# SwiGLU's gate and up matrices: the low part of the first weight tile by a subtraction on VectorE in place of a negated copy and an adding transfer

## The chip, the cores and the metric

The kernel runs on one core of a Trainium2 chip. The metric is device time in microseconds (us), the median of several runs of the whole program. The profile is one further execution, taken by the hardware profiler. The engines are TensorE (PE, matmuls), VectorE (DVE), ScalarE (ACT), GpSimd (POOL) and SyncE (SP). Each engine works off its own instructions in the order in which they were queued; semaphores tie the engines together. In this kernel SP issues plain transfers between HBM (main memory) and SBUF (on-chip memory), and GpSimd issues the adding ones.

## The reference, cut to what matters

One layer of a hybrid decoder runs on 576 tokens of width 1024: a mixer (Mamba-2 and mLSTM heads), cross attention to a memory, and a SwiGLU block. The change concerns the last one:

```
u = _rms(x) * g_pre_ffn                             # 576 x 1024
f = (jax.nn.silu(u @ w_gate) * (u @ w_up)) @ w_down # hidden width 2816 = 22 tiles of 128
x = x + _rms(f) * g_post_ffn
```

All data is float32.

## The kernel before, in words

**Three products for one.** TensorE multiplies in the type float32r, which keeps fewer bits than float32. So each operand is split into a high part (a cast to float32r) and a low part (the rest, operand minus high part), and each product is made of three: high by high, high by low, low by high. In `mul` (from line 1721 on) these are lines 1725, 1726 and 1727; line 1727 is the one that reads the low part of the weights.

**Seven products for eight.** From hidden tile 4 on, the gate and up matrices are taken in pairs of tiles (j, j+1). A pair is one weight matrix of two tiles, cut in half along its 1024 inputs (columns LA and LB of an SBUF tile); the tokens are cut in halves of 288 and the inputs in halves of 512. The 2 by 2 blocks are multiplied with seven products (w = 0 to 6) after Strassen and Winograd, not eight; each is 12 matmuls. A pair therefore needs, besides the raw tiles r1 (tile j, name `raw`) and r2 (tile j+1, name `rawx`), sums and differences of their halves, each split into high and low parts:

- `load`: r2 is fetched, and the low part l1 of r1 is made in a buffer named `wacc` (two of them). Before the change: ScalarE writes the negated, rounded r1 (line 1666), and a transfer on GpSimd's queue adds r1 from HBM to it (line 1667), which leaves r1 minus its high part.
- `high1`: ScalarE casts r1 to its high part h1 (line 1671), in one of three buffers `whi`. For five pairs, marked `first`, the low part is made here by VectorE's subtraction in one of three buffers `wlo` (line 1674), and not in `load`.
- `sums`, `diffs`: VectorE forms sums and differences, in `sw` and in place in r1 and r2 (lines 1677 to 1686). Line 1686 overwrites half of r1.
- `parts2`, `place3`, `parts3`, `parts4`: high and low parts of these. `place3` takes a half tile's low part by the negated copy and the adding transfer too, into `wlo`.
- products 0 and 1 use h1, l1; 2 and 3 the sums' parts; 4 and 5 the third parts; 6 the fourth. When `parts4` is through, r1's buffer (two of them) is free for the first tile of the next pair but one.

`early` runs products 0 and 1, `mid` 2 to 4, `late` 5 and 6. Between them ScalarE copies a half-finished sum out of its PSUM bank (cc of lines 1782 and 1793, ct of line 1789), since TensorE adds the next product onto the same bank; TensorE has to wait for that copy.

**Order.** The pairs are 6 to 20 in steps of two, first gate, then up. Pairs made by `pairs` are ordered by the framework's planner, which runs a model of time over the steps and puts each engine's instructions in a fixed order. After the pairs for tiles 6 and 8, and again after those for 10, 12 and 14, comes a stage of the down projection, `down_blocks` (from line 1946 on), with four blocks of the same kind (`Down`). There the order is written out by hand: `on(t, ...)` gives every step a place t, and the steps are queued in the order of t. The stage begins while the last gate and up pair (g_ and u in the code) is still in work, and ends with the first pair of the next group. The steps of block 0 stand in one list, which the change edits. In a `Down` block `low1` (lines 1867 to 1870) makes the low part by negated copy and adding transfer, `low1v` by a subtraction on VectorE; `diff1` overwrites part of the raw tile; `high4` and `low4` are the fourth parts. The names `keep`, `plus`, `done` empty PSUM banks; L1994 and L2002 are two such copies for u, in cc and ct.

Of the kernel before, what the change touches and what calls it, by code (L numbers as in the profile page):

```python
# [12 lines left out]
F32R = mybir.dt.float32r  # L13
# [6 lines left out]
P = 128  # L20
# [96 lines left out]
def build(nc, tc, ctx, I, O):  # L117
# [4 lines left out]
    wp = ctx.enter_context(tc.tile_pool(name="weights", bufs=1))  # L122
# [548 lines left out]
    for g in range(2):  # L671
        for hb in range(2):
            dst = cpad[:, g, 4 * hb:4 * hb + 4, :].rearrange("p b t -> p (b t)")
# [5 lines left out]
    for g in range(2):  # L679
# [13 lines left out]
        for h in range(8):  # L693
            k, j = h % 2, (8 * g + h) // 2
# [125 lines left out]
    for h in range(4):  # L820
        q, k = qk[:, h, :], qk[:, 4 + h, :]
# [607 lines left out]
    def load(key, src):  # L1429
        W[key] = wp.tile([P, 1024], F32, name="raw", tag="raw", bufs=2)  # L1430
        S.dma_start(W[key], src)
# [165 lines left out]
    for n_, (key, p) in enumerate(order):  # L1597
        src = I[{"xo": "wxo", "g": "wgate", "u": "wup"}[key[0]]][key[1]]
        at_(order[n_ - 2][1] + 0.01 if n_ > 1 else -1, load, key, src)
        if key[1] == 3:  # L1600
            at_(p, cast3, n_)
            at_((0.55, 1.05)[n_], low3, n_)
        else:
            at_(p, cast, key, PRE.index(key), wx if key in (("g", 0), ("u", 0), ("g", 1)) else None)
# [40 lines left out]
    class Pair:  # L1645

        def __init__(s, j, up, dst):
            s.j, s.up, s.dst, s.first = j, up, dst, j in (10, 16) or (j, up) == (6, 1)
            s.src = I["wup" if up else "wgate"]
            s.r1 = wp.tile([P, 1024], F32, name="raw", tag="raw", bufs=2)  # L1650
            S.dma_start(s.r1, s.src[j])

        def load(s):
            s.r2 = fp.tile([P, 1024], F32, name="rawx", tag="rawx", bufs=2)
            S.dma_start(s.r2, s.src[s.j + 1])
            if s.first:
                return
            s.l1 = fp.tile([P, 1024], F32R, name="wacc", tag="wacc", bufs=2)
            s.low(s.l1, s.r1, s.j)

        def low(s, out, raw, j, c=slice(0, 1024)):

# [6 lines left out]
        def high1(s):  # L1669
            s.h1 = wp.tile([P, 1024], F32R, name="whi", tag="whi", bufs=3)  # L1670
            A.copy(s.h1, s.r1)
            if s.first:
                s.l1 = wp.tile([P, 1024], F32R, name="wlo", tag="wlo", bufs=3)
                V.tensor_tensor(s.l1, s.r1, s.h1.bitcast(F32), op=ALU.subtract)

        def sums(s):
# [163 lines left out]
    class Down:  # L1840
# [29 lines left out]
            G.dma_start(s.f1[1], I["wdown"][s.j, :, 768 * s.c - 256:768 * s.c + 512], accum_op=ALU.add)  # L1870

        def high1(s):
            if s.n == 1:
                s.f1 = s.parts()
            A.copy(s.f1[0], s.r1)

# [69 lines left out]
    def down_blocks(c, up_gate, j):  # L1946
# [4 lines left out]
        def on(t, fn, *a):  # L1951
            ev.append((t, len(ev), lambda: fn(*a)))
# [56 lines left out]
        on(2.8, up_mul, u, "z", 6, b22, False)  # L2009
        on(4.5, lambda: u.done(0, 1, u.z, ct[:, 0, :]))  # L2010

        for k, p in (("low1", -11.3), ("sum1", -11.0), ("sum2", -10.5), ("diff2", -9.9), ("high1", -7.95), ("diff1", -7.1),
                     ("high3", -6.3), ("low3", -5.5), ("high4", -4.6), ("low4", -4.1), ("high2", -1.5), ("low2", -0.7)):
            on(p, do, 0, k)
        on(-9.0, make, 1)
        on(-8.9, do, 1, "load")
# [119 lines left out]
    with tc.manual_schedule(engines={TE.engine, A.engine, V.engine, G.engine, S.engine}):  # L2136
# [4 lines left out]
        fp = ctx.enter_context(tc.tile_pool(name="ffn", bufs=1, reuse_waits="tile"))  # L2141
# [7 lines left out]
    w_of = lambda j: weights(("d", j), I["wdown"][j, :, 0:512], 512, cut=512)  # L2149
    down_chunk(0, 4, [(j, i) for j in range(8) for i in (1, 0)], pp[1], w_of, ev_first)  # L2150
    made = down_blocks(1, pairs((6, 8), operand, whole=False), 10)
    made = down_blocks(2, pairs((10, 12, 14), operand, None, made, False), 16)
    hh, hl = SL0("hh2"), SL(2, "hl2", F32R)
    f2 = SL(4, "f_ffn")
# [257 lines left out]
```

## Time and profile before

| what | value |
|---|---|
| median of 3 runs | 1135.39 us (1132.99 to 1137.53) |
| the profiled execution | 1135.51 us, of which its span 1133.7 us |
| mean granted TensorE clock | 0.994 |
| TensorE matmuls busy | 1101.4 us, 97% of the span |
| VectorE busy | 758.1 us, 67% |
| ScalarE busy | 618.7 us, 55% |
| GpSimd busy | 233.9 us, 21% |
| pairs 6 on and down blocks | about 803 to 1077 us of the span |

By stretches of that part, from the view of windows (the first numbers are the window and its length; then the busy time with the number of instructions of PE, PEld, DVE, ACT and POOL; then the mean granted TensorE clock, the share of time in which the DMA engines were busy, and GB/s):

```
803.00:864.00 61.00, 57.36 (x425) 56.05 (x425) 39.53 (x69) 37.83 (x70) 6.85 (x8) 1.00 0.66 165
864.00:918.00 54.00, 51.59 (x382) 50.34 (x380) 40.45 (x73) 28.70 (x50) 12.03 (x14) 1.00 0.78 171
918.00:974.00 56.00, 52.74 (x382) 52.04 (x383) 41.75 (x81) 36.62 (x68) 5.96 (x7) 0.97 0.58 134
974.00:1038.00 64.00, 59.34 (x436) 57.62 (x435) 45.48 (x81) 34.19 (x59) 13.01 (x16) 0.99 0.84 210
1038.00:1077.00 39.00, 38.78 (x273) 38.78 (x274) 24.47 (x45) 23.91 (x42) 4.26 (x5) 0.92 0.52 116
```

How to read the rows of a timeline: start in us, duration, engine, line of the code, operation, output<-inputs, shapes, count, and in brackets the idle time of the engine just before with what ended it ("[3.16 <-ACT cc L1793]": 3.16 us idle, until ScalarE's instruction of line 1793 on cc was through). Matmuls overlap in the pipeline, so their durations exceed their spacing; TensorE's speed is read from the starts. The clock is a share of full speed.

### The profile page before, as it was taken

Reading aid. Unit: us, or ns where it says so; the run is one execution under the profiler, and the core shown is the slowest. Engines: PE = TensorE matmul, PEld = TensorE weight load, DVE = VectorE, ACT = ScalarE, POOL = GpSimd, SP = SyncE. Lnnn points to the kernel's source line nnn. Section 1 sums busy time; section 2 is a strip of 40 time slices with the busy share of each in tenths; the row PEclk is TensorE's granted clock in tenths of the full one; section 3 lists DMA queues with packets and bytes.
Section 4 is the critical chain, followed back from the end, with each engine's and each line's share of the span. In section 5 each row is a group of like instructions: output and inputs, shape, how many; then the busy total and the mean of one; then the engine's idle time right before and its main releaser. Section 6 shows DMA issues by size and latency. Waiting matters only on the chain.

```text
span 1133.7 us, 21313 instructions
## 1 busy us (share of the span) xinstructions
PE 1101.4 (97%) x8355; PEld 1047.8 (92%) x8355; DVE 758.1 (67%) x1508; ACT 618.7 (55%) x1143; POOL 233.9 (21%) x322
## 2 busy tenths in 40 slices
PE   9999999999999999999999999999999999998997
PEld 8999889898998999999988889999998989998997
DVE  6796874457777775659654545684577767775655
ACT  6877533356554475656454445544665566555644
POOL 1333443313122212100244202100011211121000
PEclk9999999999999999999999999999999999998999
DMA  6685555544563448753567765723764974597542
GB/s 207 161 167 128 135 163 168 149 106 126 168 181 105 129 158 294 265 209 96 200 214 251 275 209 180 254 84 104 211 140 88 224 170 122 117 249 180 129 139 84
DMA packets 62456, 191.00 MB, mean 168 GB/s; under 512 B 6892, under 2 KB 11116, under 8 KB 61844
## 3 DMA queue, kind: packets, MB, share of 16 engines
q1 hardware_dynamic: 44324, 142.19, 37.6%
q0 software_dynamic: 17744, 46.93, 20.8%
q8 instruction: 65, 1.06, 0.4%
q10 hardware_dynamic: 288, 0.52, 0.1%
q14 instruction: 35, 0.29, 0.1%
HBM read 160.31 MB, written 29.30 MB: 167 GB/s over the span
## 4 chain that ended last, share of the span: by engine, by line
PE 79%; DMA 9%; ACT 5%; DVE 4%; issue 2%; SPq 0%; DVEq 0%; ACTq 0%
PE ps_in L201 5%; PE ps_in L203 5%; PE ps_in L202 5%; PE ps_o L201 3%; PE ps_o L203 2%; PE ps_u L1725 2%; PE ps_o L202 2%; PE ps_u L1726 2%; PE ps_u L1727 2%; PE ps_g L1725 2%; PE ps_g L1726 2%; PE ps_g L1727 2%; PE ps_dn L1932 2%; PE ps_dn L201 2%; PE ps_dn L1931 2%; PE ps_dn L203 2%
## 5 line engine op out<-in xcount | busy, mean ns | idle before, releaser
L201 PE MATMUL ps_in<-uh,whi 128*128 128x320 f32 (+1 forms) x544 | 165.5, 304 | 0.0
L203 PE MATMUL ps_in<-uh,wlo 128*128 128x320 f32 (+1 forms) x544 | 163.0, 300 | 0.5 <-DVE wlo L188 0.5
L202 PE MATMUL ps_in<-ul,whi 128*128 128x320 f32 (+1 forms) x544 | 162.4, 299 | 0.0
L181 ACT CAST whi<-raw 128x1024 fp32r<-128x1024 f32 (+1 forms) x102 | 102.9, 1011 | 80.9 <-PE ps_in L202 19.5
L188 DVE TENSOR_TENSOR wlo<-raw,whi 128x512 fp32r<-128x512 f32 (+1 forms) x94 | 87.9, 935 | 59.6 <-ACT whi L181 58.7
L201 PEld LDWEIGHTS ps_in<-uh,whi 128*128 128x128 f32 x544 | 103.1, 190 | 2.5 <-issue 0.8
L203 PEld LDWEIGHTS ps_in<-uh,wlo 128*128 128x128 f32 x544 | 103.0, 189 | 2.4 <-issue 1.3
L202 PEld LDWEIGHTS ps_in<-ul,whi 128*128 128x128 f32 x544 | 103.2, 190 | 0.7
L1725 PE MATMUL ps_u<-b,whi 128*128 128x288 f32 x144 | 43.8, 304 | 9.6 <-ACT cc L1793 3.2
L186 POOL DMA_DIRECT2D wlo<-win x32 | 28.3, 885 | 94.6 <-ACT wlo L185 84.1
L1725 PE MATMUL ps_g<-b,whi 128*128 128x288 f32 x144 | 42.9, 298 | 1.2 <-ACT cc L1793 1.0
L1726 PE MATMUL ps_u<-b,whi 128*128 128x288 f32 x144 | 43.1, 299 | 0.0
L1726 PE MATMUL ps_g<-b,whi 128*128 128x288 f32 x144 | 42.5, 295 | 0.0
L201 PE MATMUL ps_o<-mixm_h,whi 128*128 128x256 f32 (+1 forms) x128 | 38.8, 304 | 1.7 <-ACT whi L181 1.6
L201 PE MATMUL ps_xo<-qh,whi 128*128 128x288 f32 x128 | 37.9, 301 | 1.0 <-ACT f_xo L1407 1.0
L202 PE MATMUL ps_o<-mixm_l,whi 128*128 128x256 f32 (+1 forms) x128 | 38.6, 302 | 0.0
L203 PE MATMUL ps_o<-mixm_h,wlo 128*128 128x256 f32 (+1 forms) x128 | 38.3, 303 | 0.0
L201 PE MATMUL ps_xq<-u2h,whi 128*128 128x320 f32 (+1 forms) x128 | 38.3, 303 | 0.0
L774 PE MATMUL ps_v<-wlo,uh 128*128 128x256 f32 x128 | 36.8, 291 | 1.4 <-DMA wlo<-wv 1.3
L202 PE MATMUL ps_xq<-u2l,whi 128*128 128x320 f32 (+1 forms) x128 | 38.0, 299 | 0.0
L203 PE MATMUL ps_xq<-u2h,wlo 128*128 128x320 f32 (+1 forms) x128 | 37.9, 297 | 0.0
L203 PE MATMUL ps_xo<-qh,wlo 128*128 128x288 f32 x128 | 37.9, 297 | 0.0
(779 smaller groups left out, 3933.0 us busy)
## 6 DMA issues: line engine op xcount, KB each, us to landing
raw<-win SPq DMA_DIRECT2D x35, 512.0 KB, 3.8
raw<-wout SPq DMA_DIRECT2D x17, 512.0 KB, 4.7
kva<-kc SPq DMA_DIRECT2D x16, 512.0 KB, 6.3
kva<-vc SPq DMA_DIRECT2D x16, 512.0 KB, 6.8
raw<-wxq SPq DMA_DIRECT2D x13, 512.0 KB, 3.6
raw<-wgate SPq DMA_DIRECT2D x13, 512.0 KB, 5.7
raw<-wup SPq DMA_DIRECT2D x13, 512.0 KB, 3.6
wlo<-win POOLq DMA_DIRECT2D x24, 256.0 KB, 5.5
```

Source lines behind the costliest of these rows:

```text
L181: A.copy(hi[:, :n], raw[:, :n])
L186: G.dma_start(lo[:, a:b], src[:, a:b], accum_op=ALU.add)
L188: e.tensor_tensor(lo[:, a:b], raw[:, a:b], hi[:, a:b].bitcast(F32), op=ALU.subtract)
L201: mm(ps, wh, ah, start=i == 0, stop=False)
L202: mm(ps, wh, al, start=False, stop=False)
L203: m = mm(ps, wl, ah, start=False, stop=i == len(tiles) - 1)
L774: m = mm(o, ah, lo[:, j:j + 256], start=False, stop=k == KT - 1, skip_group_check=True)
L1725: mm(ps, wh, b[0][:, k, :], start=start and k == 0, stop=False, skip_group_check=True)
L1726: mm(ps, wh, b[1][:, k, :], start=False, stop=False, skip_group_check=True)
L1727: m = mm(ps, wl, b[0][:, k, :], start=False, stop=k == 3, skip_group_check=True)
L1931: mm(ps, wh, bh, start=start and k == 0, stop=False, skip_group_check=True)
L1932: mm(ps, wh, bl, start=False, stop=False, skip_group_check=True)
```

## The change

The low part l1 of the first tile of each pair from tile 6 on is made by VectorE from the raw tile and its high part. The negated copy on ScalarE and the adding transfer of 512 KB on GpSimd's queue go for the eleven pairs that had them; only pair 4 keeps its old way (its low part is fetched ready-made). Pairs 10 and 16, gate, which are made inside the hand-written order, keep their buffer `wlo`; all others use `wacc`, among them 6, 10 and 16, up, which had `wlo` before and, no longer being `first`, are now prepared in the common order (`place3` ahead of `high1`). In the down stage, block 0 goes the same way: `low1` (place -11.3) is replaced by `low1v` (-4.2), `diff1` moves from -7.1 to -4.1, `high4` from -4.6 to -2.8, `low4` from -4.1 to -2.4, and the two buffers are taken at `high1`. The half tile in `place3` and the blocks 2 and 3 of the down stage keep the negated copy and the adding transfer.

```diff
-            s.j, s.up, s.dst, s.first = j, up, dst, j in (10, 16) or (j, up) == (6, 1)
+            s.j, s.up, s.dst, s.first = j, up, dst, not up and j in (10, 16)
...
-            if s.first:
-                return
-            s.l1 = fp.tile([P, 1024], F32R, name="wacc", tag="wacc", bufs=2)
-            s.low(s.l1, s.r1, s.j)
+            if s.j == 4:
+                s.l1 = fp.tile([P, 1024], F32R, name="wacc", tag="wacc", bufs=2)
+                s.low(s.l1, s.r1, s.j)
...
             A.copy(s.h1, s.r1)
-            if s.first:
-                s.l1 = wp.tile([P, 1024], F32R, name="wlo", tag="wlo", bufs=3)
+            if s.j > 4:
+                pool, tag, n = (wp, "wlo", 3) if s.first else (fp, "wacc", 2)
+                s.l1 = pool.tile([P, 1024], F32R, name=tag, tag=tag, bufs=n)
                 V.tensor_tensor(s.l1, s.r1, s.h1.bitcast(F32), op=ALU.subtract)
...
-            if s.n == 1:
+            if s.n < 2:
                 s.f1 = s.parts()
...
-        for k, p in (("low1", -11.3), ("sum1", -11.0), ("sum2", -10.5), ("diff2", -9.9), ("high1", -7.95), ("diff1", -7.1),
-                     ("high3", -6.3), ("low3", -5.5), ("high4", -4.6), ("low4", -4.1), ("high2", -1.5), ("low2", -0.7)):
+        for k, p in (("low1v", -4.2), ("sum1", -11.0), ("sum2", -10.5), ("diff2", -9.9), ("high1", -7.95), ("diff1", -4.1),
+                     ("high3", -6.3), ("low3", -5.5), ("high4", -2.8), ("low4", -2.4), ("high2", -1.5), ("low2", -0.7)):
```

## The prediction

> **What bounds the kernel now.** TensorE carries nearly the whole span, so I read first, for the stretch in which the changed pairs run (803 to 1077 us of the span), what TensorE waited for.
>
> ```profile
> PE ps_u L1725 <- ACT cc L1793: 3.2, 1, 3.2
> PE ps_u L1725 <- ACT ct L2002: 3.1, 2, 1.6
> PE ps_g L1725 <- ACT whi L1671: 2.5, 2, 2.1
> PE ps_u L1725 <- ACT cc L1994: 2.4, 2, 1.2
> PE ps_u L1727 <- DVE wlo L193: 1.1, 2, 0.8
> PE ps_g L1725 <- ACT cc L1793: 1.0, 2, 0.5
> PE ps_u L1725 <- ACT whi L192: 0.9, 1, 0.9
> ```
>
> The columns are the sum in us, the number of times and the longest. They come to 14.2 us, and all but 1.1 us is put down to ScalarE. ScalarE is busy for little more than half of the span, so the question is what it stood at. That is the second view, the waits of ScalarE in the same stretch:
>
> ```profile
> ACT wacc L1666 <- DMA raw<-wgate: 14.2, 6, 5.0
> ACT wacc L1666 <- DMA raw<-wup: 12.9, 5, 5.6
> ...
> ACT whi L1671 <- PE ps_g L1726: 5.2, 6, 1.1
> ```
>
> For 27.1 us, in all eleven of its uses, ScalarE stood at the negated copy of the first weight tile until that tile had arrived. The third view is the timeline around the longest wait; ScalarE first, then TensorE:
>
> ```profile
> 1036.83 1.06 ACT L1666 ACTIVATE wacc<-raw 128x1024 fp32r<-128x1024 f32 x1 [2.86 <-DMA raw<-wgate]
> 1037.79 0.38 ACT L1793 COPY cc<-ps_u 128x288 f32<-128x288 f32 x1
> ```
>
> ```profile
> 1038.22 0.61 PE L1725 MATMUL ps_u<-b,whi 128*128 128x288 f32 x1 [3.16 <-ACT cc L1793]
> ```
>
> The small copy of line 1793, which empties a bank for TensorE, stands in ScalarE's queue behind a negation that waits for a weight tile of a later pair (20, gate). The next worst is the same, with the cast of line 1671 behind the negation for (14, up):
>
> ```profile
> 915.17 1.06 ACT L1666 ACTIVATE wacc<-raw 128x1024 fp32r<-128x1024 f32 x1 [5.61 <-DMA raw<-wup]
> ...
> 916.80 1.03 ACT L1671 CAST whi<-raw 128x1024 fp32r<-128x1024 f32 x1
> ```
>
> ```profile
> 917.88 0.61 PE L1725 MATMUL ps_g<-u3h,whi 128*128 128x288 f32 x1 [2.08 <-ACT whi L1671]
> ```
>
> The smaller waits in the pairs (0.4 us of line 1671, 0.9 of line 192, 0.8 of line 193) lie within 5 us behind two more such stands:
>
> ```profile
> 829.35 1.06 ACT L1666 ACTIVATE wacc<-raw 128x1024 fp32r<-128x1024 f32 x1 [3.32 <-DMA raw<-wup]
> ...
> 1015.48 1.06 ACT L1666 ACTIVATE wacc<-raw 128x1024 fp32r<-128x1024 f32 x1 [5.03 <-DMA raw<-wgate]
> ```
>
> So what ends last at these places is a load, but not because the matmuls need it: the copy was queued too early.
>
> The fourth view is the granted clock behind the two long waits:
>
> ```profile
> 917.90:921.30 3.40, 3.40 (x14) 3.40 (x15) 2.99 (x5) 2.92 (x7) 0.85 (x1) 0.50 0.95 146
> 921.30:924.70 3.40, 3.40 (x28) 3.40 (x27) 2.81 (x5) 1.71 (x3) 0.00 (x0) 1.00 0.97 216
> ...
> 1038.20:1044.10 5.90, 5.88 (x24) 5.88 (x25) 2.42 (x5) 3.14 (x5) 1.68 (x2) 0.50 0.78 128
> ```
>
> The first pair of numbers is the window and its length, the next TensorE's busy time with its matmuls, the last three the clock, the DMA share and GB/s. Behind each long wait TensorE ran at 0.50: 14 matmuls in 3.40 us and 24 in 5.90 us.
>
> **The change, part by part: the pairs.** Eleven pairs (6 gate; 8, 12, 14, 18 and 20, gate and up) lose the negation (1.06 us of ScalarE each) and the adding transfer on GpSimd's queue, and gain one subtraction on VectorE, queued behind the cast. Its price is measured, since five pairs do it already:
>
> ```profile
> L1674 DVE TENSOR_TENSOR wlo<-raw,whi x5: 1219/1224/1226, 819.4 to 1011.1; 128x1024 fp32r<-128x1024 f32 x5
> ```
>
> That is 1.22 us, or 13.5 us for the eleven. With the negation goes the only step of ScalarE that reads a first tile as soon as it lands. Its next reader is the cast of line 1671, which must have one of three high-part buffers, and the row of 5.2 us above shows it waiting for TensorE to give one up. So the cast is paced by TensorE and comes late enough: the tile of (20, gate) was there at 1036.83, and its cast ran at 1052.55. I take all waits in the pairs as gone: 3.2 + 2.5 + 1.1 + 0.9 = **7.7 us**.
>
> The clock goes with them. Waits of up to 1.6 us in the first table were followed by no half clock, those of 2.1 and 3.2 us were. The normal pace is read below: 26 matmuls from 1052.11 to 1055.55, 0.132 us each. So the half clock cost 3.40 - 14 x 0.132 = 1.55 us and 5.90 - 24 x 0.132 = 2.73 us, together **4.3 us**. The Trainium skill, TensorE: Matmul & The Clock Gate, section on HAM oscillation, gives as the practical rule that the clock is lost behind idle gaps above about 3.4 us; by it these two waits would have cost no clock, and the sum would be 4.3 us smaller. The trace disagrees: a wait of 2.08 us stands right before a window at 0.50.
>
> What pays for it is VectorE. Whether the subtraction is in time is read at an undisturbed pair, 20 gate:
>
> ```profile
> 1052.55 1.03 ACT L1671 CAST whi<-raw 128x1024 fp32r<-128x1024 f32 x1
> ```
>
> ```profile
> 1053.62 0.69 DVE L1686 TENSOR_TENSOR raw<-raw,sw 128x512 f32<-128x512 f32 x1 [0.82 <-ACT whi L1671]
> ```
>
> ```profile
> 1052.11 0.30 PE L1725 MATMUL ps_g<-b,whi 128*128 128x288 f32 x1
> ...
> 1055.55 0.29 PE L1727 MATMUL ps_g<-u3h,wacc 128*128 128x288 f32 x1
> ```
>
> The cast is done at 1053.6, and VectorE, idle before, takes its next step at once. The subtraction would take that place and end at 1053.62 + 1.22 = 1054.84; the first matmul that reads it is the last row, at 1055.55. The slack is 0.71 us. Behind it the difference of line 1686 starts 1.22 us later, and with it the steps that end in freeing the raw buffer for the next load; this load has over 10 us to spare (1036.83 against 1052.55). Where VectorE is fullest:
>
> ```profile
> 930.50:941.60 11.10, 11.10 (x87) 11.10 (x85) 10.17 (x21) 7.84 (x14) 1.71 (x2) 1.00 0.67 164
> ```
>
> its third pair of numbers is 10.17 us of 11.10; one subtraction more makes 11.39, 0.3 us too many. Elsewhere it has room. Between nothing (all within the slack) and 13.5 us (all on the path) I take 1.5 us: 0.3 here and 0.1 for each pair, near the lower end because of the undisturbed pair's row. The removed transfers free GpSimd's queue and DMA time; I count nothing for that. Pairs 6, 10 and 16, up, take their low part from the two wacc buffers instead of the three wlo buffers, and their place3 comes ahead of the cast: its half-tile negation and transfer need r2 and a wlo buffer, of which one more is now free, so nothing.
>
> **The heads of the two down blocks.** Here the order is written by hand. Block 0's negation (line 1869, place -11.3) goes, its transfer with it; its subtraction comes at -4.2 on VectorE, and the in-place difference that would overwrite its source moves behind it, from -7.1 to -4.1. The step high4 moves behind the ct copy, low4 with it. The head before:
>
> ```profile
> 852.33 0.84 ACT L1869 ACTIVATE wlo<-raw 128x768 fp32r<-128x768 f32 x1 [1.12 <-PE ps_g L1727]
> 853.08 0.38 ACT L1994 COPY cc<-ps_u 128x288 f32<-128x288 f32 x1
> ```
>
> ```profile
> 857.33 0.44 ACT L1736 ACTIVATE gt<-gt 128x288 f32<-128x288 f32 x1 [1.39 <-DVE gt L1735]
> 857.68 0.49 ACT L1912 CAST u3h<-raw 128x384 fp32r<-128x384 f32 x1
> 858.08 0.39 ACT L2002 COPY ct<-ps_u 128x288 f32<-128x288 f32 x1
> ```
>
> ```profile
> 853.51 0.40 PE L1725 MATMUL ps_u<-b,whi 128*128 128x288 f32 x1 [1.22 <-ACT cc L1994]
> ...
> 858.52 0.40 PE L1725 MATMUL ps_u<-b,whi 128*128 128x288 f32 x1 [1.55 <-ACT ct L2002]
> ```
>
> The negation waits for a low-part buffer, and the copy that TensorE needs (line 1994) stands behind it. Without it that copy can run before TensorE asks for it: 1.22 us gone. At worst it still stands behind the casts that VectorE feeds, now 1.22 us later; ScalarE's idle 1.12 us and the negation's 0.84 make 1.96 us, so at least 0.7 us is left. The second wait ends on a chain that starts with the first copy (853.08 to 858.08) and loses only the cast of line 1912, 0.40 us from its start to the ct copy's; low3 there waits for its own cast, so moving the difference away from it gives nothing. So one head gains between 0.7 + 0.4 = 1.1 us and 1.22 + 1.55 = 2.8 us; I take the middle, 1.9, because VectorE is fuller here than in the undisturbed pair. Two heads: **3.8 us**. The added subtraction (768 of 1024 columns, 0.9 us as an estimate from 1.22) lies behind line 1735 and ahead of products that TensorE reaches some 2 us later: nothing, or the same 0.9 us twice if that cover is gone.
>
> **The sum**, on the profiled execution (span 1133.7, time 1135.51, within 0.2 us of the median): 7.7 + 4.3 + 3.8 - 1.5 = 14.3 us, so **1121.2 us**.
>
> **Rivals.** *Half of it.* Most steps of the pairs are placed by a planner, not by hand, and it plans anew. New waits of about half the sum appear, behind VectorE or a buffer: pairs give 12.0 - 1.5 - 3 = 7.5, the heads their least, 2.2, less 1 for late products there: 8.7 us, 1126.8. For it: the full window above; against: the undisturbed pair.
>
> *The cast takes the negation's place.* If the planner queues line 1671 as early as the negation was, ScalarE stands as before and only the heads gain: 1131.7. Against it is that the cast needs a buffer which TensorE frees late.
>
> *VectorE becomes the bound.* The Trainium skill, Perfetto Trace Analysis, section on optimizing Scalar and DVE operations, advises moving work from a saturated VectorE to ScalarE; this change goes the other way. As a mechanism here: the subtraction stands behind another of 1024 columns (line 193, priced like line 1674 at 1.22) and three half-tile steps like line 1686 (0.69 each), 3.29 us, at each of eleven pairs. TensorE then waits 3.29 - 0.71 = 2.58 us at each third matmul, 28.4 us, against 15.8 gained: 12.6 us slower, 1148.1. It decides from 15.8 / 11 + 0.71 = 2.1 us of lateness. VectorE has that much queue only at the windows like the full one, so it is unlikely in all eleven.
>
> **How the numbers follow.** Forecast 0.62, half of it 0.21, the cast in its place 0.11, VectorE as the bound 0.06. The best ends (12.0 + 5.6) give 1117.9 and the spread of the three runs reaches 2.4 us below their median: low 1115.5. Upward the range takes in the half and goes to 1131, just short of the third case. A measurement here can tell about 0.5%, 5.7 us, from no change: faster is the first two cases and a little of the third, 0.85; the same 0.09; slower 0.06.
>
> **What would show it.** Right: no line 1666 on wacc, ScalarE's 27.1 us gone with nothing like it on line 1671, no window at 0.50 in this stretch, TensorE's waits there down from 14.2 to some 4 us, with lines 2002 and 1793 left. Wrong: line 1671 waiting for raw, or line 1727 waiting for line 1674 at many pairs.

## The result and the profile after

The kernel after took 1121.09 us (median of 4 runs, 1117.70 to 1122.39), the kernel before 1136.3 us (4 runs on the same chip): a ratio of 0.9866, 95% interval 0.9834 to 0.9898. On another chip, later, it was 1122.51 against 1135.22 us. The forecast of 1121.2 us holds, but the experiments changed half of its reason. Of one experiment below (the kernel before without the adding transfers) only the times are used, since its profiled execution had a granted clock of 0.652.

The waits of TensorE in the stretch of the pairs and the down blocks (780 to 1065 us of the span after; the cast of line 1671 is line 1670 here, the subtraction is line 1674, and from line 1677 on the numbers are those of before; the columns are the sum, the number of times and the longest):

```profile
PE ps_g L1725 <- ACT cc L1793: 1.0, 2, 0.5
PE ps_dn L1931 <- ACT hop L1760: 0.8, 2, 0.4
```

Of 14.2 us 1.8 are left: the 1.0 us of line 1793 stood there before, the 0.8 us of line 1931 are new. The waits of ScalarE in the same stretch, the longest and the cast's own:

```profile
ACT hop L192 <- DVE gt L1742: 9.7, 8, 2.3
ACT hop L1760 <- DVE gt L1611: 8.3, 8, 2.4
...
ACT whi L1670 <- PE ps_g L1726: 7.4, 8, 1.0
```

In the pairs no row names a load any more (further down stand 2.5 and 1.1 us at loads of the down matrix): the 27.1 us at the negated copy are gone, and the cast, now the first reader of a raw tile, waits for TensorE to give up a buffer. The clock, by the view of windows over the five parts of the stretch (window and length, PE, PEld, DVE, ACT, POOL busy, clock, DMA share, GB/s):

```profile
814.00:846.00 32.00, 32.00 (x245) 32.00 (x244) 24.14 (x39) 19.49 (x33) 2.60 (x3) 1.00 0.45 126
846.00:894.00 48.00, 46.99 (x345) 45.55 (x344) 40.88 (x79) 27.56 (x52) 7.82 (x9) 1.00 0.65 153
894.00:949.00 55.00, 55.00 (x419) 55.00 (x417) 46.07 (x80) 33.72 (x60) 6.07 (x7) 1.00 0.53 127
949.00:997.00 48.00, 46.98 (x345) 45.52 (x344) 40.56 (x78) 27.85 (x53) 7.83 (x9) 1.00 0.66 153
997.00:1060.00 63.00, 63.00 (x478) 63.00 (x477) 47.52 (x80) 37.45 (x65) 6.22 (x8) 1.00 0.62 166
```

TensorE is busy without a break in the pairs, the clock is 1.00 in every part, and only the down blocks (second and fourth row) lose 1 us each.

Over a whole run the times scatter by some 0.3% (the standard deviation of 27 runs of the kernel before), so the experiments are also read by a stretch that every profile has: from the cast of the first tile of (6, gate) to that of (20, up), the first and the last of the sixteen. ScalarE's timeline before, and after:

```profile
808.39 1.05 ACT L1671 CAST whi<-raw 128x1024 fp32r<-128x1024 f32 x1
...
1063.33 1.05 ACT L1671 CAST whi<-raw 128x1024 fp32r<-128x1024 f32 x1 [0.99 <-PE ps_g L1726]
```

```profile
808.42 1.05 ACT L1670 CAST whi<-raw 128x1024 fp32r<-128x1024 f32 x1 [0.84 <-PE ps_dn L202]
...
1045.56 1.05 ACT L1670 CAST whi<-raw 128x1024 fp32r<-128x1024 f32 x1 [0.98 <-PE ps_g L1726]
```

That is 254.9 us before and 237.1 after; a second profile of the kernel after gave 237.2, so this measure repeats to 0.1 us where nothing waits. The profiles differ by 17.8 us here and in their spans (1133.7 and 1115.9), the medians by only 15.2 and 12.7. The profiled execution after was the shortest of its four runs (1117.7 us), and that of before began the stretch earlier than all others but one (808.4 us; the thirteen usable profiles begin it between 807.8 and 815.2). So its time probably stood at the median because a short first part hid a stretch that lost more than usual; a second profile of the kernel before, which would settle this, was not taken.

### The profile page after: what moved, and what is told of

It reads as the page before. It is cut to its first block, busy times and chain, and to the rows that moved or that the text cites. A ratio compares the mean times of both kernels' runs of the same rounds, so it can differ in the third digit from the quotient of the medians.

```text
span 1115.9 us, 21276 instructions
## 1 busy us (share of the span) xinstructions
PE 1095.6 (98%) x8355; PEld 1043.4 (94%) x8355; DVE 771.4 (69%) x1521; ACT 609.8 (55%) x1130; POOL 223.5 (20%) x309
## 3 DMA queue, kind: packets, MB, share of 16 engines
q8 instruction: 65, 1.06, 0.4%
## 4 chain that ended last, share of the span: by engine, by line
PE 81%; DVE 6%; DMA 6%; ACT 5%; issue 2%; SPq 0%; DVEq 0%; ACTq 0%; POOLq 0%
PE ps_in L201 5%; PE ps_in L203 5%; PE ps_in L202 5%; PE ps_g L1725 3%; PE ps_g L1726 3%; PE ps_g L1727 3%; PE ps_u L1726 2%; PE ps_u L1725 2%; PE ps_u L1727 2%; PE ps_o L201 2%; PE ps_o L203 2%; PE ps_o L202 2%; PE ps_dn L201 2%; PE ps_dn L203 2%; PE ps_dn L1932 2%; PE ps_dn L202 2%
## 5 line engine op out<-in xcount | busy, mean ns | idle before, releaser
L202 PE MATMUL ps_xo<-ql,whi 128*128 128x288 f32 x128 | 37.6, 295 | 0.0
```

The lines of the kernel that those rows point to most:

```text
L202: mm(ps, wh, al, start=False, stop=False)
```

## The experiments

All results in one table: the median, the difference to the kernel before in the same set of runs (1135.1, 1137.4 and 1135.2 us in the three sets), and the stretch, worked out from the two casts as above.

| kernel | median us | less before | stretch us |
|---|---|---|---|
| before | | | 254.9 |
| after (its own set; again) | 1121.1; 1122.5 | -15.2; -12.7 | 237.1; 237.2 |
| change in the pairs only | 1125.9 | -9.2 | 241.9 |
| change in the heads only | 1131.4 | -3.8 | 244.6 |
| after + one column negated early | 1120.2 | -14.9 | 238.3 |
| after + adding transfers | 1124.0 | -11.1 | 240.7 |
| after + one column + transfers | 1127.7 | -9.7 | 242.1 |
| after + full negation early | 1121.0 | -16.4 | 237.3 |
| after + full negation + transfers | 1129.9 | -5.3 | 252.7 |
| before without the transfers | 1128.8 | -6.4 | no profile |
| before, negation on GpSimd | 1143.6 | +8.3 | 259.9 |
| after, subtraction twice | 1129.3 | -8.1 | 246.3 |
| after, place3 by VectorE too | 1122.6 | -14.8 | 238.1 |

**The two parts of the change, each alone.** The first kernel is the one after with the old list of places in the down blocks, the second the one before with the new list.

```diff
-            if s.n < 2:
+            if s.n == 1:
...
-        for k, p in (("low1v", -4.2), ("sum1", -11.0), ("sum2", -10.5), ("diff2", -9.9), ("high1", -7.95), ("diff1", -4.1),
-                     ("high3", -6.3), ("low3", -5.5), ("high4", -2.8), ("low4", -2.4), ("high2", -1.5), ("low2", -0.7)):
+        for k, p in (("low1", -11.3), ("sum1", -11.0), ("sum2", -10.5), ("diff2", -9.9), ("high1", -7.95), ("diff1", -7.1),
+                     ("high3", -6.3), ("low3", -5.5), ("high4", -4.6), ("low4", -4.1), ("high2", -1.5), ("low2", -0.7)):
```

> The changed kernel with the head of the down stage put back as it was (negated copy and adding transfer of block 0 at -11.3, diff1 at -7.1, high4 at -4.6, low4 at -4.1); the pairs stay changed. The theory of the standing copy: each head has a wait of its own, so the two waits of lines 1994 and 2002 come back, 1.2 and 1.6 us twice, less the 0.6 us that the new wait at line 1931 costs now: 4.5 us of the 15.2 are lost, about 1125.5 us, and no window at half clock. Rival (the gain comes from the removed traffic, of which the heads hold only two transfers of 384 KB against eleven of 512 KB): at most 2 us are lost, 1121 to 1123 us.

> The kernel before with the new head of the down stage alone; the pairs keep the negated copy and the adding transfer. The theory of the standing copy: the heads' waits go, 4.5 us, the waits of 2.1 and 3.2 us in the pairs and the half clock behind them stay: about 1131.8 us. With the pairs alone it should add up to the whole gain. Rival (traffic): 1134 to 1136 us.

Measured: pairs only 1125.88 us, ratio 0.9927 (0.9900 to 0.9954); heads only 1131.36 us, ratio 0.9976 (0.9952 to 1.0000). TensorE's waits with the pairs only:

```profile
PE ps_u L1725 <- ACT ct L2002: 3.1, 2, 1.6
PE ps_u L1725 <- ACT cc L1994: 2.4, 2, 1.2
PE ps_g L1725 <- ACT cc L1793: 1.0, 2, 0.5
```

The pairs' waits are gone, the heads' two are as before. Both times are as expected, and the parts add up: 9.2 and 3.8 us make 13.0, beside 12.7 and 15.2 for both. With the heads only, the first two rows of the same view:

```profile
PE ps_g L1725 <- ACT whi L1671: 3.1, 1, 3.1
PE ps_g L1727 <- DMA wacc<-wgate: 2.7, 1, 2.7
```

These are other waits than in the profile of before, with the pairs' code unchanged: the loss in the pairs is not the same from run to run.

**Is it the place in ScalarE's queue?** The kernel after, and in `load` a negation of one column of the first tile, at the place of the old one: ScalarE stands there as before, for 0.2 us of work. VectorE's subtraction still makes the low part. (`early1` holds for the eleven pairs; the lines left out, here and in the next four edits, keep `high1` from taking the buffer a second time.)

```diff
+            s.early1 = s.j > 4 and not (s.j in (10, 16) or (s.j, s.up) == (6, 1))
+            if s.early1:
+                s.l1 = fp.tile([P, 1024], F32R, name="wacc", tag="wacc", bufs=2)
+                A.activation(s.l1[:, 0:1], s.r1[:, 0:1], AF.Copy, scale=-1.0)
...
```

> The changed kernel, with one more instruction of ScalarE for each of the eleven pairs: where the negated copy of the whole first tile stood, it negates a single column of it into the same buffer (which VectorE's subtraction overwrites later). There is no adding transfer and next to no work for ScalarE, but its queue stands at the load again. The theory of the standing copy: ScalarE waits some 20 to 27 us at this line for raw, the waits of TensorE at lines 1670, 1793 and 192 come back, with half clock behind the long ones: 9 to 13 us of the pairs' 14 are lost, 1130 to 1134 us. Rival (traffic, or the work of 1.06 us that ScalarE no longer has): 1121 to 1123 us.

Measured: 1120.19 us, ratio 0.9885 (0.9844 to 0.9926), no slower than the kernel after. ScalarE stood there for some 16 us in all, and TensorE's waits grew by one of 0.9 us. So the forecast's reason, "the copy was queued too early", does not seem to stand by itself. One limit: with so short a negation the planner puts the copy cc for (18, up) ahead of the stand at (20, gate), so the longest wait of before could not come back here. The kernel with the full negation, below, has the copy behind the stand again.

**Is it the traffic?** The kernel after with the eleven adding transfers of 512 KB back on GpSimd's queue, into a buffer that GpSimd clears, and GpSimd waiting for the load in ScalarE's stead.

```diff
...
+                G.memset(s.l1.bitcast(F32), 0.0)
+                G.tensor_tensor(s.l1[:, 0:1], s.r1[:, 0:1], s.r1[:, 1:2], op=ALU.subtract)
+                G.dma_start(s.l1, s.src[s.j], accum_op=ALU.add)
...
```

> The changed kernel, with the adding transfer of 512 KB put back for each of the eleven pairs, into the buffer that VectorE's subtraction overwrites later; a one-column instruction of GpSimd that reads the first tile stands ahead of it, so that GpSimd's queue waits for the load as it did before. ScalarE has none of it. The theory of the standing copy: the loads land later and GpSimd stands, but nobody in TensorE's chain waits for that: 1121 to 1124 us. Rival (the transfers slowed the loads, and that was the cost): most of the pairs' 14 us come back, 1131 to 1136 us.

Measured: 1124.02 us, ratio 0.9917 (0.9886 to 0.9948), about 3 us slower than the kernel after. Most of it is the experiment's own doing:

```profile
PE ps_g L1734 <- DVE wacc L1681: 2.0, 3, 1.1
```

Line 1681 is VectorE's subtraction here, which must wait until the transfer has left its buffer. So the transfers alone do not make the pairs' loss either.

**Both, with little work, and the full work without the transfers.** The first has the one-column negation and, behind it, the transfer; the second the full negation of 1.06 us and no transfer.

```diff
...
+                G.memset(s.l1.bitcast(F32), 0.0)
+                A.activation(s.l1[:, 0:1], s.r1[:, 0:1], AF.Copy, scale=-1.0)
+                G.dma_start(s.l1, s.src[s.j], accum_op=ALU.add)
...
```

```diff
...
+                A.activation(s.l1, s.r1, AF.Copy, scale=-1.0)
...
```

> The kernel after, with both halves of the old way put back in small form for the eleven pairs: ScalarE negates one column of the first tile as soon as it is there (0.2 us of work, but the place in its queue at which it stands until the tile has landed), and behind it a transfer of 512 KB on GpSimd's queue adds the tile from HBM to a cleared buffer. VectorE's subtraction still makes the low part and overwrites that buffer. Theory now: neither half costs much alone (e3_touch 1120.2 against 1121.1, e4_traffic 1124.0), the two together do, because the adding transfers make the loads land late and the stand then lasts until the copies that TensorE waits for. Then 1131 to 1136 us, ScalarE standing at the one-column copy for over 22 us, waits for lines 1793 or 1670 of 2 us and more on TensorE. Rival, the halves only add: 1123 to 1125, stand about 16 us as in e3_touch.

> The kernel after, with ScalarE's negation of all 1024 columns back at its old place for the eleven pairs (1.06 us each, 11.7 us in all), without the transfer; VectorE's subtraction overwrites what it wrote. Theory (stand and transfers together make the loss): loads land as early as in e3_touch, so 1120 to 1124 us and waits of TensorE of at most 3 us in the stretch. Rival, ScalarE's 11.7 us of work is what cost the time: 1128 to 1133.

Measured: 1127.68 us, ratio 0.9921 (0.9896 to 0.9946), for the first; 1121.01 us, ratio 0.9850 (0.9824 to 0.9875), for the second. The second is as expected: 11.7 us of work and the stand, here with the copy cc behind it at (20, gate) as before the change, cost nothing. The first falls between the two expectations, ScalarE stands for 20.5 us in place of the expected 22 and more, TensorE's added waits are again mostly those of line 1681, and none reaches 2 us. It can't decide alone: with the short negation the copy cc again stands ahead of the negation of (20, gate).

**All of the old way, with the subtraction on top.** So the last step was the kernel after with `s.low(s.l1, s.r1, s.j)` in `load` for the eleven pairs, negation and transfer in full. And from the other side, the kernel before without the transfers: TensorE reads the negated copy as it is, so the addition is left out of the computation.

```diff
...
+            if s.early1:
+                s.l1 = fp.tile([P, 1024], F32R, name="wacc", tag="wacc", bufs=2)
+                s.low(s.l1, s.r1, s.j)
...
```

```diff
-            s.low(s.l1, s.r1, s.j)
+            if s.j == 4:
+                s.low(s.l1, s.r1, s.j)
+            else:
+                A.activation(s.l1, s.r1, AF.Copy, scale=-1.0)
```

> The kernel after with the whole old way put back for the eleven pairs, the full negation on ScalarE (1.06 us) and the adding transfer behind it, and VectorE's subtraction on top, which overwrites the buffer. It adds to e8_both only ScalarE's work behind the stand (1.06 in place of 0.20 us). Theory (all three together): 1130 to 1136 us, a wait of TensorE of 1 to 3 us behind the stands of pairs 14, up, and 20, gate. Rival, the parts only add up (e9_neg_alone nothing, e4_traffic 3 us): 1123 to 1126.

> The kernel before without the eleven pairs' adding transfers of the first tile: the negated copy stays at its place on ScalarE and TensorE reads it as it is, so the addition of the tile is left out of the computation. ScalarE's queue is nearly the same as before. Theory now (the stand, the transfers that make loads land late, and ScalarE's work behind the stand make the loss only together): loads land 1 to 2 us sooner, ScalarE's stand falls from 27 us to some 15, TensorE's long waits for lines 1671 and 1793 go: 1124 to 1128 us. Rival, the place in ScalarE's queue is the cause by itself, as the prediction had it: 1133 to 1137.

Measured: 1129.88 us, ratio 0.9967 (0.9942 to 0.9992), for the whole old way on top, 7.4 us slower than the kernel after in the same set; 1128.83 us, ratio 0.9953 (0.9927 to 0.9980), for the kernel without transfers. The first is just under the expected window, the second just over it; the rivals (1123 to 1126, and 1133 to 1137) are further off. TensorE's waits in the first:

```profile
PE ps_u L1730 <- ACT cc L1798: 3.2, 1, 3.2
PE ps_g L1732 <- DVE wacc L1679: 2.1, 3, 0.8
PE ps_u L1730 <- ACT whi L192: 2.1, 1, 2.1
PE ps_g L1730 <- ACT whi L1674: 2.0, 1, 2.0
```

The 3.2 us at the copy cc and the 2.0 us at the cast are the two long waits of before, come back (lines are five or three higher here); the wait for the cast of line 192 was 0.9 us before. Line 1679 is again the subtraction that waits for the transfer: these 2.1 us are the experiment's own. This profile is of the longest of ten runs (1138.4 us), so it shows the mechanism, not its usual size. The place before (20, gate), without the transfers (the kernel with the full negation), SP's load and ScalarE:

```profile
1021.41 0.33 SPq L1651 DMA_DIRECT2D raw<-wgate  x1
...
1025.04 1.06 ACT L1662 ACTIVATE wacc<-raw 128x1024 fp32r<-128x1024 f32 x1 [1.48 <-DMA raw<-wgate]
1026.01 0.38 ACT L1798 COPY cc<-ps_u 128x288 f32<-128x288 f32 x1
```

And with them (the whole old way on top):

```profile
1033.91 0.33 SPq L1651 DMA_DIRECT2D raw<-wgate  x1
...
1040.85 1.06 ACT L1669 ACTIVATE wacc<-raw 128x1024 fp32r<-128x1024 f32 x1 [4.18 <-DMA raw<-wgate]
1041.81 0.38 ACT L1798 COPY cc<-ps_u 128x288 f32<-128x288 f32 x1
```

The same instructions stand in the same order here and at (12, up); at (8, gate) and (18, up) the planner's order differs between the two kernels. The load takes 3.63 us from its issue until the negation can start in the one, 6.94 us in the other, and the copy behind it is late by that. TensorE's wait for the copy is 0.65 and 3.19 us:

```profile
1026.44 0.40 PE L1730 MATMUL ps_u<-b,whi 128*128 128x288 f32 x1 [0.65 <-ACT cc L1798]
```

```profile
1042.24 0.40 PE L1730 MATMUL ps_u<-b,whi 128*128 128x288 f32 x1 [3.19 <-ACT cc L1798]
```

The load of (12, up), which holds up the cast of (12, gate), goes the same way: 4.35 and 3.93 us in the two kernels of the stand without the eleven transfers (one column and full), 6.62 before, and 7.80, 6.95 and 6.22 in the three others that have stand and transfers (heads only, one column, full). Over all eleven places the time from the load's issue to the negation is 4.4 and 4.2 us on average without the transfers, and 5.2 to 5.4 in the four kernels with them. At some places, (14, up) and (20, up) above all, the two groups differ by some 0.5 us or less.

**The stand moved to GpSimd.** The kernel before, with the eleven negations on GpSimd's queue ahead of their transfers.

```diff
...
+                G.tensor_scalar(s.l1, s.r1, -1.0, None, op0=ALU.mult)
+                G.dma_start(s.l1, s.src[s.j], accum_op=ALU.add)
```

> The kernel before with the eleven negations moved from ScalarE to GpSimd's queue, ahead of their adding transfers: all transfers stay, ScalarE neither stands nor works for them, GpSimd stands. Theory: the pairs' 10 to 14 us come back nearly whole, as far as the low parts are in time; a negation on GpSimd should take at least the 1.08 us that its clearing of the same buffer took in e4_traffic, perhaps twice that: 1124 to 1129 us. Rival, the transfers and the late loads cost TensorE the time whoever stands: 1131 to 1137.

Measured: 1143.55 us, ratio 1.0096 (1.0072 to 1.0120): slower than before, as neither theory had it. GpSimd's group and the waits of TensorE (sum, times, longest):

```profile
L1662 POOL TENSOR_SCALAR wacc<-raw 128x1024 fp32r<-128x1024 f32 x11 | 31.9, 2898 | 91.9 <-DMA raw<-wgate 54.3 <-PE ps_g L1731 11.0 <-DMA raw<-wup 10.6
```

```profile
PE ps_g L1731 <- DMA wacc<-wgate: 13.3, 3, 6.3
PE ps_u L1729 <- ACT ct L2006: 3.1, 2, 1.6
PE ps_u L1729 <- ACT cc L1998: 2.4, 2, 1.2
```

The long waits for ScalarE's cc and cast are gone, as the theory had it, though the transfers run. But a negation takes 2.90 us here against 1.06 us on ScalarE, and three low parts arrive up to 6.3 us late. This suggests why the old way negated early: a low part made through a transfer must start long before it is read. A later place in ScalarE's own queue, with the transfer kept, was not tried.

**How much cover has VectorE?** The kernel after with the subtraction issued twice: sixteen times 1.22 us, 19.6 us more.

```diff
                 V.tensor_tensor(s.l1, s.r1, s.h1.bitcast(F32), op=ALU.subtract)
+                V.tensor_tensor(s.l1, s.r1, s.h1.bitcast(F32), op=ALU.subtract)
```

> The kernel after, with VectorE's subtraction of the pairs made twice (sixteen pairs, 16 x 1.22 = 19.6 us more on VectorE). Theory: the subtraction lies in the cover of TensorE's first products, with some 0.7 us to spare at an undisturbed pair, so a second one is late by about 0.5 us at some pairs: 1121 to 1125 us. Rival, VectorE is already on the path and the change got its gain in spite of that: up to 19.6 us, 1135 to 1141.

Measured: 1129.28 us, ratio 0.9925 (0.9907 to 0.9944), that is 4.6 to 7.1 us slower than the kernel after, by the differences to before; the stretch is 9.1 us longer. Between the two expectations, nearer to the first. The pair in which it is late, VectorE and then TensorE:

```profile
1037.12 1.23 DVE L1674 TENSOR_TENSOR wacc<-raw,whi 128x1024 fp32r<-128x1024 f32 x1 [0.50 <-ACT whi L1670]
1038.27 0.45 DVE L1743 TENSOR_TENSOR gt<-gt,ps_u 128x288 f32<-128x288 f32 x1
1038.63 1.22 DVE L1675 TENSOR_TENSOR wacc<-raw,whi 128x1024 fp32r<-128x1024 f32 x1
```

```profile
1038.77 0.40 PE L1726 MATMUL ps_u<-u3h,whi 128*128 128x288 f32 x1 [1.09 <-DVE gt L1743]
...
1039.90 0.61 PE L1728 MATMUL ps_u<-u3h,wacc 128*128 128x288 f32 x1 [0.61 <-DVE wacc L1675]
```

The extra work makes both the step of line 1743 and the low part late, 1.7 us here. The first subtraction was covered; a second one would not be.

**The rest of the transfers.** The kernel after with `place3`'s half tile made by VectorE too, behind its cast; no adding transfer is left in the pairs from tile 6 on.

```diff
-            s.low(s.l3[:, LA], s.r2[:, LB], s.j + 1, LB)
+            if s.j == 4:
+                s.low(s.l3[:, LA], s.r2[:, LB], s.j + 1, LB)
...
+            if s.j > 4:
+                V.tensor_tensor(s.l3[:, LA], s.r2[:, LB], s.h3[:, LB].bitcast(F32), op=ALU.subtract)
```

> The kernel after, with the half-tile low part of place3 also by VectorE's subtraction (behind the cast of its half, 0.69 us each, sixteen pairs from tile 6 on), so that no negated copy and no adding transfer is left in these pairs. Theory: with 1.8 us of waits left in the stretch there is little to gain: 1119 to 1122 us. Rival, the rest of the adding transfers (256 KB each) still delays the loads and costs time elsewhere: below 1118. Rival, the added half tile on VectorE comes late: above 1124.

Measured: 1122.57 us, ratio 0.9881 (0.9848 to 0.9913), just above the expected window and the kernel after's time within the scatter. With 1.8 us of waits left there was little to take, and the 11 us more of VectorE (sixteen times 0.69) lie beside other work.

**The kernel after once more**, on the chip of the last set:

> The kernel after, unchanged, on the chip of these runs: 1118 to 1123 us, so that the distance of the three others to it is measured on one chip.

Measured: 1122.51 us, ratio 0.9900 (0.9868 to 0.9932).

## Why the prediction was right, point by point

**What ScalarE stood at.** Right as a reading, half right as a cause. "What ends last at these places is a load, but not because the matmuls need it: the copy was queued too early" names one of two conditions. ScalarE standing at the load cost nothing where the eleven adding transfers did not run; the transfers alone cost some 3 us, mostly by the experiment's own subtraction. Together they cost 7.4 us by the medians and 15.6 us of the stretch in the one profile, some 2 us of it again the experiment's own. The cleanest pair is the full negation on top without and with the transfers: by their distances to before, in two sets of runs, the transfers cost 11.1 us there (16.4 less 5.3), against 1.6 to 4.1 us without the stand. The change removes both at once, so the sum did not suffer from the wrong reason: that much of the hit is luck. "The removed transfers free GpSimd's queue and DMA time; I count nothing for that" was the wrong half: without the transfers the kernel before gains 6.4 us (2.3 to 8.3 by its interval) of the 9.2 us that the pairs are worth. How the transfers delay a load, by the DMA engines or on the way from HBM, was not tried and stays open. One name was wrong as well, there and in an expectation: the tile called (14, up) is (12, up), and what waits behind its negation is the cast of (12, gate).

**Pairs.** Put at 12.0 us of gain (7.7 of waits, 4.3 of clock). By the starts of TensorE's matmuls in the two profiles the three parts outside the heads give 14.2 us (with the heads 18.7; the casts, which begin the stretch 0.9 us differently, give 17.8). Each stop costs some 0.15 us more than its row says (ahead of the wait of 3.16 us two matmuls began at 1034.63 and the next at 1038.22, 3.59 - 2 x 0.132 = 3.32 us too late), and VectorE took nothing of it. By the medians it is less: 9.2 us for the kernel with the pairs only, probably because the profiled execution of before lost more there than usual. The two errors, a sum too low for its profile and a profile that lost more than the median, cancel in the forecast. That is luck too.

**The clock.** The two windows at 0.50 are gone, as forecast. The reasoning from the length of the wait fell: with the heads only, a wait of 3.06 us left the clock alone.

```profile
915.35 0.40 PE L1725 MATMUL ps_g<-u3h,whi 128*128 128x288 f32 x1 [3.06 <-ACT whi L1671]
```

```profile
915.30:918.80 3.50, 3.45 (x24) 3.29 (x25) 3.05 (x5) 3.21 (x7) 0.85 (x1) 1.00 0.90 151
```

And with the subtraction twice, stops of no more than 1.1 us were followed by half clock:

```profile
1039.80:1043.20 3.40, 3.30 (x14) 3.30 (x15) 3.40 (x7) 0.83 (x3) 0.00 (x0) 0.51 0.38 63
```

The Trainium skill, TensorE: Matmul & The Clock Gate, has beside the rule of gaps above about 3.4 us a second case, in its section on a second HAM failure mode: a clock that falls with short gaps when they come often. The row of 3.06 us fits the rule; that of 0.51 behind stops of 1.1 and 0.6 us is nearer to the second case, though two stops are not many; the single waits of 2.1 and 3.2 us of the kernel before fit neither. So the 4.3 us were a term with a chance, not a sure one.

**VectorE's cost.** Put at 1.5 us for the pairs, nearest to nothing; measured, nothing. No wait for the subtraction stands in the view after. At (20, gate), the pair that the forecast worked out, VectorE after, then TensorE's first reader:

```profile
1035.54 1.23 DVE L1674 TENSOR_TENSOR wacc<-raw,whi 128x1024 fp32r<-128x1024 f32 x1 [1.52 <-ACT whi L1670]
1036.80 0.69 DVE L1686 TENSOR_TENSOR raw<-raw,sw 128x512 f32<-128x512 f32 x1
```

```profile
1037.79 0.29 PE L1727 MATMUL ps_g<-u3h,wacc 128*128 128x288 f32 x1
```

Done at 1036.77 and read at 1037.79: 1.0 us to spare, where 0.71 was forecast. The kernel with two subtractions shows that this was all there was.

**Heads.** Put at 3.8 us; 2.25 and 2.23 us by TensorE's starts in the two profiles, 4.5 together; by the medians 3.8 us for the kernel with the heads only, and 3.5 to 6.0 as what the whole change gives beyond the pairs. Both old waits went whole, 3.1 us a head, a little more than the forecast's upper bound of 2.8. Some 0.8 us a head is lost again at line 1931 (the row of 0.4 us and the matmuls right behind it), to the cast of line 1760, which the forecast did not name. That cast waits for VectorE's sums of line 1611, the second row of ScalarE's view: here, and not at the subtraction, VectorE comes next.

**The rivals.** "Half of it" needed new waits of half the sum: two rows of 0.4 us came. "The cast takes the negation's place" would show line 1670 waiting for a load: it waits for TensorE. "VectorE becomes the bound" has its mechanism in the kernel with two subtractions, at the cost of 4.6 to 7.1 us.

## What to carry to other kernels

An instruction that reads a load as soon as it lands makes its whole in-order queue as late as that load. Whether this costs anything is set by how late the load can get, so look at the transfers beside it too, and test the stand and the traffic both apart and together. Before a sum is built on one profile, compare the part of the profile that carries it with a second execution: here the time stood at the median while the stretch probably did not. And when work moves to a busier engine, measure the cover by doubling the work there: once was free, twice was not.

## What the runs showed of the hardware

- A 512 KB load landed 3.6 to 4.4 us after its issue without the adding transfers near it, and 5.3 to 7.9 us with them, at the two places followed above (read to the start of the negation that waits for it). They are not the only thing that delays one: in the kernel with one column negated early, without them, the load of (18, gate) took 7.5 us (1003.31 to 1010.82), and its wait of 0.9 us came of that.
- A negated copy of 128x1024 took 1.06 us on ScalarE and 2.90 us on GpSimd, and VectorE's subtraction of that size 1.22 us.
- Half clock is not told by the length of one wait: the 2.08 us of the kernel before were followed by it, the 3.06 us of the kernel with the heads only were not. In the kernel with the old way on top, behind waits of 1.96 and 0.73 us within 1.3 us:

```profile
923.00:926.50 3.50, 3.50 (x18) 3.50 (x17) 3.47 (x6) 1.75 (x5) 0.00 (x0) 0.53 0.95 179
```
